# Six Strassen pairs in the last mLSTM heads and eight in the attention of a two-layer encoder trunk

## The chip, the cores and the metric

The kernel runs on one core of one Trainium2 chip. The metric is device time in microseconds (us) of one launch. Five engines run their own instruction streams in order and meet at semaphores: TensorE (PE in the profile, with its weight loads as PEld), VectorE (DVE), ScalarE (ACT), GpSimd (POOL, unused here) and SyncE (SP), whose queue issues every DMA of this kernel.

## The reference

One sequence of 512 tokens, width 2048, float32, passes two layers. Each layer normalises, modulates by a condition vector `c`, mixes, gates, projects back and adds a gated, normalised residual.

```python
# layer 0: mLSTM, 8 heads, dk 256, dv 512; w_in 2048 x (2*2048 + 3*4096 + 16)
qk = silu(causal_conv(proj[..., :A_V0], conv_w, conv_b))        # q and k, 8 heads x 256 each
ht = mlstm_chunkwise(q, k, v, li, lf)                           # gated linear attention
y = sigmoid(o) * rmsnorm_per_head(ht, g_head) * silu(z)
x = x + gate * rmsnorm(y @ w_out, g_post)                       # w_out 4096 x 2048
# layer 1: band attention, 16 heads x 128, K and V from the stream after layer 0
kv = modulated(rmsnorm(x, kv_g)) @ kv_w                         # 2048 x 4096
qz = modulated(rmsnorm(x, g_pre)) @ b_w_in                      # 2048 x 4096: queries and gate z
o = chunk_band_attention(q, k, v, rel_table)                    # softmax(q k / sqrt(128) + bias)
x = x + gate * rmsnorm((o * silu(z)) @ w_out, g_post)           # 2048 x 2048
```

## The kernel before

**Arithmetic.** All products are float32 made of float32r matmuls. `split` (L181 on ACT, L182 on DVE) cuts a float32 tile into a rounded high part (`wh` for weights) and the rest (`wl`). `mm3` issues three matmuls, high x high, high x low and low x high, so one 128 x 128 weight block costs three matmuls per 256 or 512 tokens.

**Weights.** `stream()` lists the weight matrices as pieces of up to 128 x 1024 floats, in the order of use. `wpiece` loads the next piece into `wr` (tag `raw`, two buffers, a third from a pool named in `spare` in some stages), then splits it into `wh` and `wl` (three buffers each). Loads, splits and results are traced with a priority 300 instructions ahead; a planner in the framework then fixes one order for each engine and inserts the semaphores. A tile pool has so many buffers for a tag; an instruction that writes a tile whose buffer is still read waits for the last reader.

**Seven products.** `proj_s` computes two column tiles c1, c2 of 128 outputs each, from 16 row tiles of 128 taken as eight pairs. For a pair the 2 x 2 grid of weight blocks meets two row tiles and two halves of 256 tokens. The plain way (`eight` in the code) takes 4 x `mm3` of 512 tokens, 12 matmuls. Strassen's way in Winograd's form (`seven`) takes 7 x `mm3` of 256 tokens, 21 matmuls, with sums of weight blocks and sums of token halves as operands. The argument `f` says how many of the eight pairs go the Strassen way; the rest go the plain way. Four PSUM tiles D, C, A, B collect the products, and an evacuation (L313 on ACT, L314 to L322 on DVE) adds them up into z1 and z2; PSUM has five such tiles, so the next tile's C, A and B take over the buffers of the last tile's D, C and A.

**Sums of weights.** For each Strassen pair `wpiece` computes on DVE L206, L207 (in place, in the raw tile) and L208 into `ws`, and splits `ws` into `wsh` and `wsl`. A piece holds either one Strassen pair and one plain pair, or two Strassen pairs. With `merged=True` two pairs share one `ws` tile of 768 columns (keys and attention); without it each pair has its own of 384 (heads). `bufs=(2, 3)` in the heads means two buffers of `ws` and three of `wsh` and `wsl`; a `wsh` buffer is free again when PE has finished the A product of its pair.

**Stages.** From 0 to about 243 us the condition vector, the norms and the projections of the first heads (`lead`, `ps_l`) run together. Heads 0 to 3 of the mLSTM use plain projections, with sums for the condition (L381) on DVE in the background. From head 4 (`HALF`) the o and z columns go through `proj_s` with `RAMP = [4, 5, 5, 5]` pairs, one number for each of the four tiles, while `head_sums` builds the token sums; heads 5, 6 and 7 use `HEAD_PAIRS = 5` for q, k and the four o/z tiles, six tiles a head. A head runs q tile, k tile, v (plain), four o/z tiles. Its end, the products `ps_n` with v, the squares, a reciprocal of a 128 x 512 tile (L737) and four multiplies (L739), runs beside the q tile of the next head. `nm` is a row of gate values broadcast over partitions (L655), read by L657 and by the exponentials L601 and L603; `v3` is the fourth quarter of v, read by the last `ps_n` matmul of each group.

Then come `a_w_out`, the residual, K and V (`proj_s` for K with 6, 7 and then 8 pairs, merged, sums in pool `zp`), and the inputs `h2`, with `three_sums` for each Strassen pair of the attention. The attention loop has one `proj_s` for each of 16 heads with `ATT_PAIRS = 7`, giving q (scaled, split into `q`) and the gate z (`z`, two buffers holding both). At the third piece `mid()` runs for older heads: `mixed(h-2)` (products with v, `ps_o`; result times z, L1046; store to `y2c`), `weights(h-1)` (scores `ps_s`, bias and maximum L1010, exponentials L1011, reciprocal L1012, scaling L1013) and the loads `fetch_k(h + 1)`, `fetch_v(h)` on SP. K of a head is split into `k` at the end of `queries`, and its first 128 columns are read as they are by the first score matmul of `weights`. Last comes `b_w_out` and the second residual.

Of the kernel before, what the change touches and what calls it, by code (L numbers as in the profile page):

```python
# [9 lines left out]
F32 = mybir.dt.float32  # L10
F32R = mybir.dt.float32r
# [4 lines left out]
P = 128  # L16
D = 2048
S = 512
# [9 lines left out]
BH = 16  # L28
# [12 lines left out]


KEY_PAIRS = [6, 7, 8, 8, 8, 8, 8, 8]
HEAD_PAIRS = 5
RAMP = [4, 5, 5, 5]
HALF = NH // 2
ATT_PAIRS = 7


def pair_pieces(f, merged=False):  # L50
# [82 lines left out]
def hybrid_trunk(ctx, tc, xT, xN, c, adaT, cols, wst, wg, ext, kc, out):  # L133
    nc = tc.nc
# [8 lines left out]
    def pool(name, bufs=1, **kw):  # L143
        return tc.tile_pool(name=name, bufs=bufs, reuse_waits="tile", **kw)
# [9 lines left out]
    ksc = [dram.tile([P, 2, S], F32, name=f"ksc{i}") for i in range(BH // 2)]  # L154
    vsc = [dram.tile([P, 4, S], F32, name=f"vsc{g}") for g in range(4)]
# [24 lines left out]
    def split(hi, lo, src):  # L180
        nc.scalar.copy(hi, src)  # L181
        nc.vector.tensor_tensor(lo, src, hi.bitcast(F32), op=ALU.subtract)  # L182
# [82 lines left out]
    def proj_s(mat, xs, ss, f, z1, z2, name, pl, bufs, at={}, merged=False):  # L265


        D, C, A, B = [newp(f"ps_{n}{name}") for n in "dcab"]
        pieces = pair_pieces(f, merged)
        begun = set()  # L270
        h0, h1_ = slice(0, 256), slice(256, 512)
        for i, (sk, nk) in enumerate(pieces):
            if i in at:
                at[i]()
            main, *extra = wpiece(mat, [len(ks) for ks in sk], pl, bufs)

            def acc(ps, cols, parts, b, x, last):
                start = id(ps) not in begun
                begun.add(id(ps))
                w = slice(b * P, (b + 1) * P)  # L280
                mm3(ps[:, cols], parts[0][:, w], parts[1][:, w], x[:, 0, :], x[:, 1, :], start, last)

            def eight():
                b0 = 4 * sum(len(ks) for ks in sk)
                for m, k in enumerate(nk):
                    for j in range(2):
                        for t, ps in enumerate((A, B)):
                            acc(ps, slice(0, S), main, b0 + 4 * m + 2 * j + t, xs[2 * k + j], False)

            def seven(g, ks):  # L290
                ns = len(ks)
                b0 = 4 * sum(len(u) for u in sk[:g])
                end = i == len(pieces) - 1 and g == len(sk) - 1
                for ps, cols, t, at_, x, last in (
                    (D, h1_, 0, 1, lambda k: ss[k][1], False),
                    (D, h0, 0, 0, lambda k: xs[2 * k][:, :, h0], end),
                    (C, h0, 1, 1, lambda k: ss[k][2], False),
                    (C, h1_, 1, 0, lambda k: ss[k][0], end),
                    (A, h0, 0, 3, lambda k: xs[2 * k + 1][:, :, h0], False),
                    (A, h1_, 1, 2, lambda k: xs[2 * k + 1][:, :, h1_], end),  # L300
                    (B, h0, 0, 2, lambda k: ss[k][3], end),
                ):
                    if i == 0 and g == 0 and ps is B:
                        eight()
                    for j, k in enumerate(ks):
                        acc(ps, cols, extra[g] if t else main, (0 if t else b0) + at_ * ns + j, x(k), last and j == ns - 1)

            if i:
                eight()
            for g, ks in enumerate(sk):  # L310
                seven(g, ks)
        with tc.high_priority(AHEAD):
            nc.scalar.copy(z1[:, 0, :], D[:, h0])  # L313
            nc.vector.tensor_tensor(z2[:, 1, :], z1[:, 0, :], D[:, h1_], op=ALU.add)  # L314
            nc.vector.tensor_tensor(z1[:, 1, :], z2[:, 1, :], C[:, h0], op=ALU.add)
            nc.vector.tensor_tensor(z2[:, 0, :], z2[:, 1, :], C[:, h1_], op=ALU.add)
            nc.vector.tensor_tensor(z2[:, 1, :], z1[:, 1, :], C[:, h1_], op=ALU.add)
            nc.vector.tensor_tensor(z1, z1, A.rearrange("p (a t) -> p a t", a=2), op=ALU.add)
            if f < KT // 2:
                nc.vector.tensor_tensor(z2, z2, B.rearrange("p (a t) -> p a t", a=2), op=ALU.add)  # L320
            else:
                nc.vector.tensor_tensor(z2[:, 0, :], z2[:, 0, :], B[:, h0], op=ALU.add)  # L322
# [37 lines left out]


    phA = ExitStack()
    tp = phA.enter_context(pool("t1", bufs=4, side="right"))
    mst = ExitStack()
    q1p = mst.enter_context(pool("q1", side="right"))
    ap_ = mst.enter_context(pool("ada", side="right"))
# [5 lines left out]
    sp = spare[0] = st.enter_context(pool("start"))  # L372
# [19 lines left out]
        return [ada_load(k, j, sp, 4) for j in range(2)] + [ada_load(KT + k, j, ap_, ADA_BUFS) for j in range(2)]  # L392

    pin = tc.keep_in_program_order
    crow = [tp.tile([P, S], F32, tag="t", name=f"crow{i}")[0:1] for i in range(4)]
    for i in range(4):
        pin(nc.sync.dma_start(crow[i], c[i * S : (i + 1) * S].unsqueeze(0)))
    xt, xq = [], []
# [1 line left out]
    for q in range(4):  # L400
        t = sp.tile([P, 4, S], F32, name=f"xt{q}")
# [44 lines left out]
    h1 = []  # L446
# [27 lines left out]
    hp = hst.enter_context(pool("head"))  # L474
# [98 lines left out]
    h1s = []  # L573
# [9 lines left out]

    def pair(c, name, f=HEAD_PAIRS, at={}):
        z1, z2 = (acp.tile([P, 2, 256], F32, tag="so", name=f"{name}_{i}", bufs=6) for i in range(2))
        proj_s("a_w_in", h1, h1s, f, z1, z2, name, hq, (2, 3), at)
        return [z.rearrange("p a t -> p (a t)") for z in (z1, z2)]

    def scores(h, j, qk, pr, nm, nmd, tot):
# [30 lines left out]
    for h in range(NH):  # L620
# [20 lines left out]
        if h == HALF:  # L641
# [5 lines left out]
            hq = hqst.enter_context(pool("hq", side="right"))  # L647
# [25 lines left out]
        for m in range(4):  # L673
            with tc.high_priority(AHEAD):
                if m < 3:
                    t = hp.tile([P, 2, S], F32R, tag="qk", name=f"v{h}_{m}", bufs=4)
                    split(t[:, 0, :], t[:, 1, :], pv[m])
                else:
                    t = hp.tile([P, S], F32, tag="v3", name=f"v{h}_{m}")
                    nc.scalar.copy(t, pv[m])  # L680
            v.append(t)
        if h < HALF:
# [239 lines left out]
    rst.close()  # L922
    zst = ExitStack()
    zp = zst.enter_context(pool("zp", bufs=2, side="right"))
    for i in range(KT // 2):
        z = zp.tile([P, 4, 256], F32, tag="z", name=f"zk{i}")
        ready = len(hs)
        at = {2: input_sums} if ready < KT // 2 else {}
        assert ready == KEY_PAIRS[i]
        spare[0] = zp  # L930
        proj_s("kv_w", hkv, hs, ready, z[:, 0:2, :], z[:, 2:4, :], f"k{i}", zp, (2, 2), at, True)
        nc.sync.dma_start(ksc[i].rearrange("p a t -> p (a t)"), z.rearrange("p a t -> p (a t)"))
    kst.close()
    ast = ExitStack()
    kq = ast.enter_context(pool("kq"))
# [26 lines left out]
    bias = at.tile([P, S], F32, name="bias")  # L962
    nc.vector.memset(bias[:64, 448:512], NEG)

    def fetch(h, ts, src, tag):
        ts.append(at.tile([P, S], F32, tag=tag, name=f"{tag}{h}", bufs=2))
        nc.sync.dma_start(ts[h], src)

    def fetch_k(h):
        fetch(h, kt, ksc[h // 2][:, h % 2, :], "kt")  # L970

    def fetch_v(h):
        fetch(h, vt, vsc[h // 4][:, h % 4, :], "vt")

    fetch_k(0)

    def queries(h, steps):

        z = at.tile([P, 4, 256], F32, tag="z", name=f"z{h}", bufs=2)
        proj_s("b_w_in", h2, h2s, ATT_PAIRS, z[:, 0:2, :], z[:, 2:4, :], f"z{h}", kq, (2, 2), steps, True)  # L980
        qz = z.rearrange("p a t -> p (a t)")
        nc.scalar.mul(qz[:, :S], qz[:, :S], P**-0.5)
        q = at.tile([P, 2, 384], F32R, tag="q", name=f"q{h}", bufs=2)
        split(q[:, 0, :], q[:, 1, :], qz[:, P:S])
        sz = qz[:, S:]
        nc.scalar.activation(sz, sz, AF.Silu)
        k = at.tile([P, 2, S], F32R, tag="kk", name=f"k{h}")
        split(k[:, 0, :], k[:, 1, :], kt[h])
        b0 = bsc[h]
        for p0, n in ((0, 448), (64, S)):  # L990
            src = bass.AP(b0.tensor, b0.offset + P - 1 + p0 * (EXTW - 1), [[EXTW - 1, 64], [1, n]])
            nc.sync.dma_start(bias[p0 : p0 + 64, :n], src)
        return (qz[:, :P], q, k), sz

    def weights(h, q0, q, k):

# [53 lines left out]
    for h in range(BH + 2):  # L1050

        def turn():
            if h > 1:
                pts[h - 2] += flipped(h - 2, prs.pop(h - 2), (2, 3))
                vs[h - 2] = split_v(h - 2)

        def mid():
            if h > 1:
                mixed(h - 2, pts.pop(h - 2), vs.pop(h - 2), szs.pop(h - 2))
            if 0 < h <= BH:  # L1060
                prs[h - 1] = weights(h - 1, *qs.pop(h - 1))
            if h < BH - 1:
                fetch_k(h + 1)
            if h < BH:
                fetch_v(h)

        if h < BH:
            qs[h], szs[h] = queries(h, {1: turn, 2: mid})
        else:
            turn()  # L1070
            mid()
        if 0 < h <= BH:
            pts[h - 1] = flipped(h - 1, prs[h - 1], (0, 1))
# [105 lines left out]
```

## Time and profile before

| quantity | value |
|---|---|
| three runs | 2814.0, 2814.4, 2812.62 us; median 2814.0 us |
| the profiled execution's own time | 2812.05 us, 1.75 us more than its span |
| its span, first to last instruction | 2810.3 us |
| mean granted TensorE clock | 0.998 |
| busy PE / DVE / ACT | 2777.9 / 2059.0 / 1330.2 us |
| attention, one head | 25.24 us, start to start |

A row of a timeline gives start, duration (us), engine, source line, operation, output <- input, shapes and how many; in square brackets the idle time before it and what ended it. Matmuls overlap, so the distance of two starts is the cost, not the duration. A row of a window gives for each engine its busy time and its instructions. A row of the waits gives the sum of a wait, how often, and the longest.

### The profile page before, as it was taken

Reading aid. Unit: us, or ns where it says so; the run is one execution under the profiler, and the core shown is the slowest. Engines: PE = TensorE matmul, PEld = TensorE weight load, DVE = VectorE, ACT = ScalarE, POOL = GpSimd, SP = SyncE. Lnnn points to the kernel's source line nnn. Section 1 sums busy time; section 2 is a strip of 40 time slices with the busy share of each in tenths; the row PEclk is TensorE's granted clock in tenths of the full one; section 3 lists DMA queues with packets and bytes.
Section 4 is the critical chain, followed back from the end, with each engine's and each line's share of the span. In section 5 each row is a group of like instructions: output and inputs, shape, how many; then the busy total and the mean of one; then the engine's idle time right before and its main releaser. Section 6 shows DMA issues by size and latency. Waiting matters only on the chain.

```text
span 2810.3 us, 40423 instructions
## 1 busy us (share of the span) xinstructions
PE 2777.9 (99%) x15308; PEld 2420.7 (86%) x15308; DVE 2059.0 (73%) x3473; ACT 1330.2 (47%) x1955; POOL 0.2 (0%) x4
## 2 busy tenths in 40 slices
PE   7999999999999999999999999999999999999998
PEld 5787888888888989989988888888998899999887
DVE  7986978868689776856867445567985788889625
ACT  4234524234334554444635344568534466666523
POOL 0000000000000000000000000000000000000000
PEclk9999999999999999999999999999999999999999
DMA  8875687868774332332323656788535534334635
GB/s 300 299 257 182 222 319 242 307 221 285 263 241 154 106 113 90 110 100 99 109 91 133 223 195 209 256 265 298 176 129 173 171 123 127 120 127 127 229 102 171
DMA packets 177371, 524.33 MB, mean 187 GB/s; under 512 B 19044, under 2 KB 37508, under 8 KB 176664
## 3 DMA queue, kind: packets, MB, share of 16 engines
q1 hardware_dynamic: 177176, 521.75, 55.0%
q8 instruction: 120, 1.97, 0.3%
q14 instruction: 75, 0.61, 0.1%
HBM read 488.07 MB, written 38.85 MB: 187 GB/s over the span
## 4 chain that ended last, share of the span: by engine, by line
PE 89%; DVE 5%; DMA 3%; issue 2%; ACT 1%; SPq 0%; DVEq 0%; ACTq 0%
PE ps_y L223 18%; PE ps_v L223 10%; PE ps_o L223 6%; PE ps_z L223 5%; PE ps_azo L223 4%; PE ps_qk L223 4%; PE ps_az L223 4%; PE ps_bzo L223 3%; PE ps_l L223 3%; PE ps_kv L223 3%; PE ps_cz L223 3%; PE ps_dz L223 3%; PE ps_bz L223 2%; PE ps_s L223 2%; PE ps_czo L223 2%; PE ps_dzo L223 2%
## 5 line engine op out<-in xcount | busy, mean ns | idle before, releaser
L182 DVE TENSOR_TENSOR wl<-wr,wh 128x1024 fp32r<-128x1024 f32 (+3 forms) x586 | 678.3, 1159 | 410.5 <-ACT wh L181 400.4
L181 ACT CAST wh<-wr 128x1024 fp32r<-128x1024 f32 (+3 forms) x586 | 585.8, 1000 | 819.1 <-PE ps_y L223 231.7
L223 PE MATMUL ps_y<-wh,y 128*128 128x512 f32 x1536 | 475.6, 390 | 0.0
L223 PEld LDWEIGHTS ps_y<-wh,y 128*128 128x128 f32 x1536 | 288.3, 188 | 59.5
L223 PE MATMUL ps_v<-wh,h 128*128 128x512 f32 x1024 | 321.7, 390 | 0.0
L181 ACT CAST wsh<-ws 128x384 fp32r<-128x384 f32 (+1 forms) x205 | 129.5, 632 | 368.7 <-issue 132.1
L223 PE MATMUL ps_y<-wl,y 128*128 128x512 f32 x768 | 299.0, 389 | 0.0
L182 DVE TENSOR_TENSOR wsl<-ws,wsh 128x384 fp32r<-128x384 f32 (+1 forms) x205 | 144.1, 703 | 122.6 <-ACT wsh L181 122.6
L223 PEld LDWEIGHTS ps_v<-wh,h 128*128 128x128 f32 x1024 | 192.2, 188 | 39.5 <-issue 0.3
L223 PE MATMUL ps_v<-wl,h 128*128 128x512 f32 x512 | 199.7, 390 | 0.0
L381 DVE CUSTOM_DVE_ANT_0 ada<-ada,scB,mod 128x1024 f32<-128x1024 f32 x128 | 163.9, 1280 | 26.1 <-DMA ada<-in_adaT 24.6
L381 DVE CUSTOM_DVE_ANT_0 ada<-ada,scB,cl 128x1024 f32<-128x1024 f32 x128 | 163.6, 1279 | 20.6 <-DMA ada<-in_adaT 20.2
L223 PEld LDWEIGHTS ps_y<-wl,y 128*128 128x128 f32 x768 | 144.2, 188 | 29.8
L223 PE MATMUL ps_kv<-wh,hkv 128*128 128x512 f32 x512 | 159.7, 391 | 0.0
L206 DVE TENSOR_TENSOR ws<-wr 128x256 f32<-128x256 f32 (+1 forms) x205 | 104.7, 520 | 30.3 <-DMA wr<-in_wst 28.3
L223 PE MATMUL ps_qk<-h,wh 128*128 128x512 f32 x384 | 119.2, 390 | 0.0
L223 PE MATMUL ps_o<-h,wh 128*128 128x512 f32 x384 | 118.2, 389 | 0.0
L223 PE MATMUL ps_z<-h,wh 128*128 128x512 f32 x384 | 118.2, 389 | 0.0
L223 PEld LDWEIGHTS ps_v<-wl,h 128*128 128x128 f32 x512 | 96.2, 188 | 19.9 <-issue 0.9
L223 PEld LDWEIGHTS ps_kv<-wh,hkv 128*128 128x128 f32 x512 | 95.9, 188 | 19.6
L223 PE MATMUL ps_l<-h,wh 128*128 128x512 f32 x320 | 99.4, 392 | 1.6 <-ACT oz L467 0.9
L223 PE MATMUL ps_kv<-wl,hkv 128*128 128x512 f32 x256 | 99.7, 389 | 0.0
(385 smaller groups left out, 5865.4 us busy)
## 6 DMA issues: line engine op xcount, KB each, us to landing
wr<-in_wst SPq DMA_DIRECT2D x520, 512.0 KB, 3.4
ada<-in_adaT SPq DMA_DIRECT2D x256, 512.0 KB, 5.8
xt<-nsc SPq DMA_DIRECT2D x46, 256.0 KB, 4.0
yr<-ysc SPq DMA_DIRECT2D x16, 512.0 KB, 3.6
wr<-in_wst SPq DMA_DIRECT2D x30, 256.0 KB, 3.8
wr<-in_wst SPq DMA_DIRECT2D x16, 384.0 KB, 5.7
bsc<-in_ext SPq DMA_DIRECT2D x16, 320.0 KB, 5.8
xt<-in_xT SPq DMA_DIRECT2D x4, 1024.0 KB, 7.0
```

The lines of the kernel that those rows point to most:

```text
L181: nc.scalar.copy(hi, src)
L182: nc.vector.tensor_tensor(lo, src, hi.bitcast(F32), op=ALU.subtract)
L206: nc.vector.tensor_tensor(t[:, : 2 * w], r[:, w : 3 * w], r[:, : 2 * w], op=ALU.subtract)
L223: nc.tensor.matmul(ps, a, b, start=start, stop=stop)
L381: pin(nc.vector.tensor_tensor_reduce(at, at, scB[:, j * D // 2 : (j + 1) * D // 2], 1.0, mod[:, i : i + 1] if j else col(CB + i), ALU.mult ...
```

## The change

`HEAD_PAIRS` goes from 5 to 6, the last two tiles of `RAMP` from 5 to 6, and `ATT_PAIRS` from 7 to 8. That is one more Strassen pair in 18 tiles of heads 5 to 7, in 2 tiles of head 4 and in 16 of the attention: 36 pairs. More token sums (`h1s`, `h2s`) must be held. Room for them is taken from: one of four buffers of pool `t1` (temporaries of the whole first layer; one of the four `crow` tiles moves to pool `start`); one of three `wsh` and `wsl` buffers in the heads; the buffer of `v3`, which now shares `nm`'s single buffer; and in the attention one of two buffers for K (`kt`), one of two for the split query (`q`), and one of two for the raw query, by cutting `z` into `zq` (one buffer) and `z` (two). K of head h is now loaded in `mid()` of head h and not of head h - 1. The weight sums of the key stage get a pool of their own (`zx`) that is closed before the last values.

```diff
-HEAD_PAIRS = 5
-RAMP = [4, 5, 5, 5]
+HEAD_PAIRS = 6
+RAMP = [4, 5, 6, 6]
 HALF = NH // 2
-ATT_PAIRS = 7
+ATT_PAIRS = 8
...
-    tp = phA.enter_context(pool("t1", bufs=4, side="right"))
+    tp = phA.enter_context(pool("t1", bufs=3, side="right"))
...
-    crow = [tp.tile([P, S], F32, tag="t", name=f"crow{i}")[0:1] for i in range(4)]
+    crow = [(tp if i < 3 else sp).tile([P, S], F32, tag="t", name=f"crow{i}")[0:1] for i in range(4)]
...
-        proj_s("a_w_in", h1, h1s, f, z1, z2, name, hq, (2, 3), at)
+        proj_s("a_w_in", h1, h1s, f, z1, z2, name, hq, (2, 2), at)
...
-                    t = hp.tile([P, S], F32, tag="v3", name=f"v{h}_{m}")
+                    t = hp.tile([P, S], F32, tag="nm", name=f"v{h}_{m}")
...
+    zxst = ExitStack()
+    zx = zxst.enter_context(pool("zx", side="right"))
...
-        proj_s("kv_w", hkv, hs, ready, z[:, 0:2, :], z[:, 2:4, :], f"k{i}", zp, (2, 2), at, True)
+        proj_s("kv_w", hkv, hs, ready, z[:, 0:2, :], z[:, 2:4, :], f"k{i}", zx, (2, 2), at, True)
...
+    zxst.close()
...
-        fetch(h, kt, ksc[h // 2][:, h % 2, :], "kt")
+        fetch(h, kt, ksc[h // 2][:, h % 2, :], "kt", 1)
...
-        z = at.tile([P, 4, 256], F32, tag="z", name=f"z{h}", bufs=2)
-        proj_s("b_w_in", h2, h2s, ATT_PAIRS, z[:, 0:2, :], z[:, 2:4, :], f"z{h}", kq, (2, 2), steps, True)
-        qz = z.rearrange("p a t -> p (a t)")
-        nc.scalar.mul(qz[:, :S], qz[:, :S], P**-0.5)
-        q = at.tile([P, 2, 384], F32R, tag="q", name=f"q{h}", bufs=2)
-        split(q[:, 0, :], q[:, 1, :], qz[:, P:S])
-        sz = qz[:, S:]
+        z1 = at.tile([P, 2, 256], F32, tag="zq", name=f"zq{h}")
+        z2 = at.tile([P, 2, 256], F32, tag="z", name=f"z{h}", bufs=2)
+        proj_s("b_w_in", h2, h2s, ATT_PAIRS, z1, z2, f"z{h}", kq, (2, 2), steps, True)
+        zq, sz = (z.rearrange("p a t -> p (a t)") for z in (z1, z2))
+        nc.scalar.mul(zq, zq, P**-0.5)
+        q = at.tile([P, 2, 384], F32R, tag="q", name=f"q{h}")
+        split(q[:, 0, :], q[:, 1, :], zq[:, P:])
...
-            if h < BH - 1:
-                fetch_k(h + 1)
+            if 0 < h < BH:
+                fetch_k(h)
```

More of the change, by code (lines that the diff above doesn't have):

```diff
@@ L963, in hybrid_trunk, with fetch @@
     nc.vector.memset(bias[:64, 448:512], NEG)
-    def fetch(h, ts, src, tag):
-        ts.append(at.tile([P, S], F32, tag=tag, name=f"{tag}{h}", bufs=2))
+    def fetch(h, ts, src, tag, bufs):
+        ts.append(at.tile([P, S], F32, tag=tag, name=f"{tag}{h}", bufs=bufs))
         nc.sync.dma_start(ts[h], src)
     def fetch_k(h):
-        fetch(h, kt, ksc[h // 2][:, h % 2, :], "kt")
+        fetch(h, kt, ksc[h // 2][:, h % 2, :], "kt", 1)
     def fetch_v(h):
-        fetch(h, vt, vsc[h // 4][:, h % 4, :], "vt")
+        fetch(h, vt, vsc[h // 4][:, h % 4, :], "vt", 2)
     fetch_k(0)
     def queries(h, steps):
-        z = at.tile([P, 4, 256], F32, tag="z", name=f"z{h}", bufs=2)
-        proj_s("b_w_in", h2, h2s, ATT_PAIRS, z[:, 0:2, :], z[:, 2:4, :], f"z{h}", kq, (2, 2), steps, True)
-        qz = z.rearrange("p a t -> p (a t)")
-        nc.scalar.mul(qz[:, :S], qz[:, :S], P**-0.5)
-        q = at.tile([P, 2, 384], F32R, tag="q", name=f"q{h}", bufs=2)
-        split(q[:, 0, :], q[:, 1, :], qz[:, P:S])
-        sz = qz[:, S:]
+        z1 = at.tile([P, 2, 256], F32, tag="zq", name=f"zq{h}")
[5 more added lines that the diff above has]
+        split(q[:, 0, :], q[:, 1, :], zq[:, P:])
         nc.scalar.activation(sz, sz, AF.Silu)
@@ L992, in queries @@
             nc.sync.dma_start(bias[p0 : p0 + 64, :n], src)
-        return (qz[:, :P], q, k), sz
+        return (zq[:, :P], q, k), sz
     def weights(h, q0, q, k):
```

## The prediction

> **What bounds the kernel now.** I read the page's busy shares first, then the chain of waits, then what PE waits for. The four fields of a window row are busy time and instruction counts of PE, PEld, DVE, ACT and POOL, then the clock, the DMA share and GB/s.
>
> ```profile
> span 2810.3 us, 40423 instructions
> ...
> PE 2777.9 (99%) x15308; PEld 2420.7 (86%) x15308; DVE 2059.0 (73%) x3473; ACT 1330.2 (47%) x1955; POOL 0.2 (0%) x4
> ...
> PE 89%; DVE 5%; DMA 3%; issue 2%; ACT 1%; SPq 0%; DVEq 0%; ACTq 0%
> ```
> ```profile
> PE ps_lead L223 <- ACT h L358: 8.9, 4, 3.4
> ...
> PE ps_az L223 <- DVE h L182: 0.8, 1, 0.8
> ```
> ```profile
> 985.00:995.00 10.00, 10.00 (x62) 8.91 (x61) 8.90 (x14) 4.17 (x7) 0.00 (x0) 1.00 0.15 53
> 995.00:1005.00 10.00, 10.00 (x75) 9.51 (x74) 9.68 (x18) 3.81 (x6) 0.00 (x0) 1.00 0.56 176
> 1005.00:1015.00 10.00, 10.00 (x64) 9.02 (x63) 9.93 (x20) 5.50 (x7) 0.00 (x0) 1.00 0.32 106
> 1255.00:1275.70 20.70, 20.70 (x143) 19.23 (x142) 12.66 (x27) 7.24 (x12) 0.00 (x0) 1.00 0.31 102
> 2107.00:2214.00 107.00, 107.00 (x580) 93.26 (x579) 66.65 (x111) 46.44 (x66) 0.00 (x0) 1.00 0.52 173
> 2301.71:2326.95 25.24, 25.24 (x193) 24.35 (x192) 22.40 (x49) 16.20 (x30) 0.00 (x0) 1.00 0.39 125
> ```
>
> PE is busy for 99% of the span and its largest wait belongs to the start. So a removed matmul is worth its full time, as long as nothing else takes PE's place. The DVE column says where something might. In an attention head (last row) DVE has 2.84 us of 25.24 left, and beside the q and k tiles of a late head (first three) only 1.49 of 30. In an o/z tile (1255) and in the last values (2107) it has room.
>
> **The matmuls saved.** The rows are starts of PE in one attention head: a piece of two Strassen pairs begins at 2285.12 and ends at 2290.16; a plain pair runs from 2293.08 to 2295.83.
>
> ```profile
> 2285.12 0.40 PE L223 MATMUL ps_dz<-h2s,wh 128*128 128x256 f32 x2
> ...
> 2290.16 0.93 PE L1023 MATMUL ps_t<-kcs,s 128*128 128x128 f32 x7
> 2290.85 0.48 PE L223 MATMUL ps_dz<-h2s,wh 128*128 128x256 f32 x2
> ...
> 2293.08 0.63 PE L223 MATMUL ps_az<-h,wh 128*128 128x512 f32 x2
> ...
> 2295.83 0.40 PE L223 MATMUL ps_bz<-h2s,wh 128*128 128x256 f32 x2
> ```
>
> Plain: 12 matmuls of 512 tokens, 2.75 us, 229 ns each. Strassen: 42 matmuls of 256 for two pairs in 5.04 us, so 21 in 2.52, 120 ns each. The gain is 0.23 us a pair, and 36 pairs give **-8.3 us** (20 in the heads -4.6, 16 in the attention -3.7). Loads and bytes of weights stay the same. The Trainium skill speaks against this change: "TensorE: Matmul & The Clock Gate", section "Back-to-back issue gap", gives a sustained spacing of about 81 ns at 128 columns and 131 ns at 512. A straight line between them is 98 ns at 256, an estimate, by which a pair would go from 1.57 to 2.06 us and 36 pairs would cost 17 us. The rows above, 229 and 120 ns, time the very matmuls and decide against that; no chance is given to it.
>
> **Attention: the single K buffer.** rows of SP, ACT and DVE in a head's middle and end, and between them the times that the 16 loads of `kt` took from issue to landing:
>
> ```profile
> 2279.74 0.38 SPq L967 DMA_DIRECT2D kt<-ksc  x1
> ```
> ```profile
> DMA to landing us min/median/max: 4.4/6.2/6.5
> ```
> ```profile
> 2282.34 0.60 ACT L181 CAST k<-kt 128x512 fp32r<-128x512 f32 x1
> ```
> ```profile
> 2283.69 0.67 DVE L182 TENSOR_TENSOR k<-kt,k 128x512 fp32r<-128x512 f32 x1
> 2284.28 0.48 DVE L1013 TENSOR_SCALAR s<-s,mx 128x512 f32<-128x512 f32 x1
> 2285.08 0.56 DVE L182 TENSOR_TENSOR wsl<-ws,wsh 128x384 fp32r<-128x384 f32 x1 [0.33 <-ACT wsh L181]
> 2285.68 0.69 DVE L206 TENSOR_TENSOR ws<-wr 128x512 f32<-128x512 f32 x1
> ...
> 2289.21 0.41 DVE L317 TENSOR_TENSOR z<-z,ps_cz 128x256 f32<-128x256 f32 x1
> ...
> 2298.82 0.41 DVE L206 TENSOR_TENSOR ws<-wr 128x256 f32<-128x256 f32 x1
> 2299.27 0.29 DVE L207 TENSOR_TENSOR wr<-ws,wr 128x128 f32<-128x128 f32 x1
> ```
>
> Before, the K issued at 2279.74 is for the next head and has a whole head to land. After, `mid()` issues it at the same place for the same head. Landing at 2285.94 (+6.2), ACT's cast cannot start at 2282.34 but ends at 2286.54. DVE, in order, has finished the softmax at about 2284.15 (2284.28 + 0.48 less the 0.6 of `k` itself), so it sits idle for 2.4 us with the split of `k`, the split of the next tile's first sums, `wl` and the evacuation L314 to L322 queued behind it; on ACT the `wsh` and `wh` casts queue too. DVE also gets more work from the eighth pair: L206, L207 and L208 and the split of the fourth piece take the wide form (0.69 for 0.41, twice 0.42 for 0.29, 0.96 for 0.56), and the last addition shrinks from 0.69 to 0.41: +0.67 us. Its cycle is 22.40 + 0.67 + 2.4 = 25.47 us, or about 25.07 if five of its short gaps close up (0.08 each, an estimate from the 0.2 to 0.33 us gaps in these rows). PE's is 25.24 - 0.23 = 25.01. DVE exceeds it by 0.06 to 0.46 us; over the 15 heads with this load 0.9 to 6.9 us. From that comes once what PE has in hand: from the start of `k` to the end of L317 took 5.9 us, 5.4 without the L1013 between, so after the cast's end at 2286.54 L317 would end near 2292.0, while the next head's A, which takes its PSUM buffer, starts 24 matmuls after 2290.85, near 2293.8: 1.8 us. The loss is 0 to 5.1; I take **+1.9**, from the middle of the excess (15 x 0.25 - 1.8), since some gaps will close.
>
> The Trainium skill's "DMA: Bandwidth & Descriptors", section "Anatomy of one DMA — SWDGE (gpsimd) path", has about 2.0 us plus bytes over 436 GB/s, for transfers issued from GpSimd: 2.6 us for these 256 KB, an estimate. By it K would be there at 2282.3, with no idle time and the full 3.7 us kept. The median of 16 landings, 6.2 us, decides for the loss.
>
> **q and k tiles of heads 5 to 7.** DVE at the end of the head before, beside the q tile:
>
> ```profile
> 993.12 3.35 DVE L737 RECIPROCAL dd<-dd 128x512 f32<-128x512 f32 x1 [0.72 <-ACT dd L736]
> ```
>
> Each of these tiles gets L206, L207, L208 and one more split: 0.41 + 0.29 + 0.29 + 0.56 = 1.55 us of DVE work. In the 30 us of the three windows above DVE has 1.49 us to spare and gets 3.1, while PE saves 0.46. A deficit of up to 2 us is partly covered by the pieces split ahead. With two `wsh` buffers, not three, that cover shrinks: the fourth piece's split must wait for PE's A product of the third piece's first pair, and if that falls behind the reciprocal, 3.35 us of DVE stand in front of it. I take 1.0 us a head between 0 (cover holds) and 2 (it doesn't): **+3.0** for three heads, 0 to 6.
>
> **o/z tiles with six pairs.** There are 14 (12 in heads 5 to 7, two in head 4). Window 1255 leaves DVE 8 us of 20.7, so 1.55 more hides. Two buffers delay the fourth piece's split behind an A product; in the order of placement D of the second piece now often stands ahead of A of the first, which gives PE other work meanwhile. I take 0.05 each between 0 and 0.2: **+0.7**.
>
> **Pool `t1`, four buffers to three.** Nothing in the trace shows this wait. Its nearest row is the wait of 8.9 us above, four times in the start, where PE isn't full. If one temporary of heads 0 to 4 came late by a 512-token DVE operation (0.68 us), twice, it would be 1.4. I take **+0.4** of 0 to 1.5; a gain is excluded, as fewer buffers release nothing earlier.
>
> **`v3` in `nm`'s buffer.** `nm` now waits on SP until the last `ps_n` of the previous head has read `v3`.
>
> ```profile
> 977.20 7.23 PE ps_n L223 x44
> ```
> ```profile
> 982.54 0.33 SPq L656 DMA_DIRECT2D ssum<-gsc  x1
> 992.43 0.33 SPq L199 DMA_DIRECT2D wr<-in_wst  x1
> ```
> ```profile
> nm<-gsc SPq DMA_DIRECT2D x8, 256.0 KB, 4.2
> ```
> ```profile
> 988.95 0.68 DVE L657 TENSOR_TENSOR nmd<-nm,maskd 128x512 f32<-128x512 f32 x1
> ```
>
> The products end at 984.43, 1.9 us after the load's place in the queue. It lands at 988.6 (+4.2), 0.3 before L657 wants it, and the next weight load on SP is not due before 992.43. **0**, at most 0.5 a head.
>
> **First attention head.** Its first piece held a plain pair of the last `h`, which is what PE waits for there (0.8 us, second of the waits quoted). That pair is gone, so **-0.5**, between 0 and -0.8. The `three_sums` that replace it are some 3 us on DVE, hidden in 2107 to 2214 with 40 us free. If the sums come last there instead, the wait stays.
>
> **Edits at nothing.** `zq` and one `q` buffer are free again in `mid()`, about 10 us before the next head writes them. The pool `zx` only ends earlier than `zp` did; its readers are long done.
>
> **Sum.** -8.3 + 1.9 + 3.0 + 0.7 + 0.4 - 0.5 = -2.8 us. The profiled execution took 2812.05 us (1.75 around its span), so 2809.2. The median of the runs lies 1.95 above that execution: **2811.2**.
>
> **The rivals.**
>
> *All hidden.* The K landing is a median under a weight load issued 1 us earlier. If it lands within 25.01 - 23.07 = 1.94 us of DVE idle, that is in 5.75 us or less (the fastest took 4.4), or if DVE's gaps close by 0.46, the attention loses nothing; if the pieces split ahead cover the q and k tiles too, what is left is -8.3 - 0.5 + 0.4 = -8.4: 2805.6. For it speaks that excess and cover are both fractions of a us; against it DVE's 9.93 of 10 us.
>
> *Slower: K becomes the bound of the attention.* The cycle is then the K load, ACT's cast and DVE's queue behind it, and each us of landing is a us per head. The other terms sum to -4.7, so it is slower than 0.2% (5.6 us) once 15e - 1.8 - 4.7 exceeds 5.6, at an excess of e = 0.81 us, a landing of 6.6 us if no gap closes, 7.0 if five do. The longest seen is 6.5. With e = 1.0: +8.5 and 2822.5. For it speaks how near 6.5 is; against it that the same queue carries the same bytes.
>
> *Slower: two `wsh` buffers stop PE in every head tile.* If PE comes to the fourth piece before its split, each q and k tile would lose its 1.55 us of new DVE work, 6 x 1.5 = 9, and each o/z tile about a split's 0.56, 14 x 0.5 = 7. With -6.5 for the rest: +9.5 and 2823.5. Against it stands DVE's room in 1255.
>
> **How the numbers follow.** The forecast (part of the gain given back) has 0.38, all hidden 0.34, K the bound 0.18, the buffers 0.10. A measurement of this kernel tells about 0.2%, 5.6 us, from no change: faster is below 2808.4, slower above 2819.6. The forecast's own range is 2808 to 2817 (K +5.1 and head tiles +6 not both at their worst), inside "same" but for its edge. So faster 0.34, same 0.38, slower 0.28. For 8 in 10 the range goes from the hidden case, 2805.0, to near the K case, 2821.5.
>
> **What the profile after would show.** 432 fewer 512-column matmuls and 756 more of 256. A head period in the attention of 25.01 us if hidden, over 25.1 if DVE sets it; an ACT wait for `kt` fifteen times, DVE idle before `k` near 2.4 us. PE waits for `wl`, `wh` or `wsl` in the q and k tiles of heads 5 to 7, and PE below 10 of 10 in those windows; no PE wait for `h` in the first attention head. I am wrong if the K wait is absent or several us longer, if PE stops in o/z tiles, or if the `t1` temporaries make PE wait in heads 0 to 4.

## The result and the profile after

| | before | after |
|---|---|---|
| median of 7 runs | 2814.0 us | 2821.9 us (2818.8 to 2826.5) |
| ratio to before | | 1.0033, 95% interval 1.0021 to 1.0045 |
| profiled execution, span | 2810.3 us | 2824.7 us |
| PE busy in the span | 99% | 98% |

The change is slower by 7.9 us, where 2811.2 us was forecast and 2821.5 was the end of the range. The profiled execution after took 2826.5 us, the slowest of its seven, so the profiles stand 14.4 us apart; a second profile of the same kernel (below) shows which part of that is chance of one execution.

The page of the kernel after:

```profile
span 2824.7 us, 41212 instructions
...
PE 2782.3 (98%) x15632; PEld 2433.5 (86%) x15632; DVE 2095.3 (74%) x3567; ACT 1348.1 (48%) x1981; POOL 0.2 (0%) x4
...
PE 81%; DVE 9%; DMA 4%; issue 3%; ACT 2%; SPq 0%; DVEq 0%; ACTq 0%
```

The matmuls went as planned (324 more in number), but the chain's share of PE fell from 89 to 81%. Where it went is seen by stage. The rows of the windows are, in both kernels: the first o/z tile of head 4 to the first product of `a_w_out`; the body of the attention (first to last product of the 16 tiles); its end (to the last product with v, beside the first products of the last projection); the last projection. Columns as in the prediction: PE, PEld, DVE, ACT, POOL, clock, DMA share, GB/s. Before:

```profile
891.57:1526.97 635.40, 633.83 (x3932) 573.77 (x3931) 453.92 (x856) 315.44 (x442) 0.00 (x0) 1.00 0.31 104
...
2221.10:2618.08 396.98, 396.22 (x3004) 382.23 (x3002) 347.05 (x751) 251.14 (x431) 0.00 (x0) 1.00 0.42 130
2618.08:2634.70 16.62, 16.42 (x92) 13.79 (x91) 14.94 (x37) 14.77 (x30) 0.00 (x0) 1.00 0.65 239
2634.70:2800.34 165.64, 165.64 (x734) 137.13 (x732) 66.36 (x77) 52.86 (x76) 0.00 (x0) 1.00 0.46 159
```

After:

```profile
890.93:1526.02 635.09, 632.28 (x4112) 579.09 (x4111) 477.72 (x940) 323.99 (x460) 0.00 (x0) 1.00 0.31 104
...
2228.13:2623.19 395.06, 392.86 (x3147) 386.51 (x3146) 350.36 (x747) 254.78 (x431) 0.00 (x0) 1.00 0.42 130
2623.19:2643.08 19.89, 18.00 (x93) 14.94 (x92) 15.60 (x37) 14.51 (x30) 0.00 (x0) 0.91 0.58 199
2643.08:2814.85 171.77, 169.36 (x733) 138.87 (x732) 67.44 (x79) 53.97 (x78) 0.00 (x0) 0.98 0.46 156
```

Of the gain forecast for the matmuls, heads 4 to 7 kept 0.3 of 4.6 us and the body of the attention 1.9 of 3.7. The end of the attention is 3.3 us longer and the last projection, which the change does not touch, 6.1. Both show a clock below 1.00. PE's waits in these three stages, and how the tile `kt` was waited for:

```profile
PE ps_t L1026 <- DVE pt L182: 1.9, 1, 1.9
PE ps_s L223 <- DVE z L1049: 1.9, 3, 1.2
PE ps_y L223 <- ACT wh L181: 1.1, 1, 1.1
PE ps_y L223 <- DVE wl L182: 0.8, 1, 0.8
PE ps_y L223 <- ACT y L181: 0.5, 1, 0.5
```
```profile
  DMA kt<-ksc: 50.2, 15
  ACT k L181: 32.7, 15
...
DMA to landing us min/median/max: 3.8/6.0/6.6
```

The first two rows of the second fence are the idle time until K landed and until ACT's part of `k` was done, and how often: ACT waits 3.3 us a head and DVE 2.2, fifteen times, close to the forecast 2.4. In the end of the attention the same wait is followed by a stop of PE (`ps_t`, 1.9 us).

**The end and the half clock.** After the last tile's K, the rows of DVE, SP and ACT in the kernel after:

```profile
2620.46 0.69 DVE L182 TENSOR_TENSOR k<-kt,k 128x512 fp32r<-128x512 f32 x1 [2.97 <-ACT k L181]
2621.41 1.23 DVE L182 TENSOR_TENSOR wl<-wr,wh 128x1024 fp32r<-128x1024 f32 x1 [0.26 <-ACT wh L181]
...
2628.20 1.48 DVE L182 TENSOR_TENSOR pt<-ps_t,pt 128x512 fp32r<-128x512 f32 x3
```
```profile
2622.67 3.43 SPq L199 DMA_DIRECT2D wr<-in_wst  x3
```
```profile
2625.97 1.05 ACT L181 CAST wh<-wr 128x1024 fp32r<-128x1024 f32 x1 [2.19 <-DMA wr<-in_wst]
```

The split `wl` of a weight piece stands behind `k` on DVE. When it ends (2622.64), SP issues the next load of weights; ACT waits 2.19 us for it, and `pt` on DVE stands behind the split of the piece that it brings. With K a head ahead (below) the same `wl` ended 2.45 us before the tile's last product, here 0.55 us. PE waits for `pt`:

```profile
2628.94 0.33 PE L1026 MATMUL ps_t<-kcs,s 128*128 128x128 f32 x1 [1.89 <-DVE pt L182]
...
2629.86 3.00 PE L223 MATMUL ps_o<-pt,vv 128*128 128x512 f32 x9
...
2641.40 1.73 PE L223 MATMUL ps_o<-pt,vv 128*128 128x512 f32 x9
```

After the stop the nine `ps_o` products take 3.00 us, a head later the same nine 1.73. The trace's record of the granted clock has 0.5 for 3.4 us from 2629.2 on, and for 6.8 us from 2670.2 on. The second follows a stop in the last projection:

```profile
2668.77 0.50 PE L223 MATMUL ps_y<-wh,y 128*128 128x512 f32 x1 [1.13 <-ACT wh L181]
2670.03 0.69 PE L223 MATMUL ps_y<-wl,y 128*128 128x512 f32 x1 [0.76 <-DVE wl L182]
```

10.2 us at half clock are up to 5.1 us of lost products, an estimate (half of the time, though PE also stood still in a part of it), where PE's waits in the end and the last projection are 4.3 us together. By these rows PE waits at the second stop for weights, `wh` and `wl`, and only 0.5 us for `y`; what brings it about is found on SP's queue. The load of the seventh `y2` tile stood directly ahead of the first load of `x2` before, at 2636.34. After, it stands behind the eight loads of `x2` and four loads of weights, 41 us after the last projection's first product (2624.2), not 17 (2619.1):

```profile
2636.34 0.32 SPq L1094 DMA_DIRECT2D y2r<-y2c  x1
```
```profile
2664.58 0.33 SPq L199 DMA_DIRECT2D wr<-in_wst  x1
2664.95 0.91 SPq L1097 DMA_DIRECT2D y2r<-y2c  x2
```

The planner, which gives each engine one order, laid out the end of the attention differently once K came late, and put this load elsewhere. The profiles of all the runs below agree: in the four profiles where the last head's K is late and this load is not moved it stands behind all of `x2`, in the eight where that K comes a head ahead it stands ahead of `x2`. That the order causes the second stop is shown by moving the load back (below).

### The profile page after: what moved, and what is told of

It is laid out like the page before. It is cut to its first block, busy times and chain, and to the rows that moved or that the text cites. A ratio compares the mean times of both kernels' runs of the same rounds, so it can differ in the third digit from the quotient of the medians.

```text
span 2824.7 us, 41212 instructions
## 1 busy us (share of the span) xinstructions
PE 2782.3 (98%) x15632; PEld 2433.5 (86%) x15632; DVE 2095.3 (74%) x3567; ACT 1348.1 (48%) x1981; POOL 0.2 (0%) x4
## 4 chain that ended last, share of the span: by engine, by line
PE 81%; DVE 9%; DMA 4%; issue 3%; ACT 2%; SPq 0%; DVEq 0%; ACTq 0%
PE ps_y L223 17%; PE ps_v L223 10%; PE ps_o L223 5%; PE ps_z L223 5%; PE ps_qk L223 4%; PE ps_kv L223 3%; PE ps_azo L223 3%; PE ps_l L223 3%; PE ps_cz L223 3%; PE ps_dz L223 3%; PE ps_az L223 2%; DVE wl L182 2%; PE ps_bzo L223 2%; PE ps_dzo L223 2%; PE ps_czo L223 2%
## 5 line engine op out<-in xcount | busy, mean ns | idle before, releaser
L181 ACT CAST wsh<-ws 128x384 fp32r<-128x384 f32 (+1 forms) x225 | 144.9, 644 | 258.0 <-issue 126.9
L182 DVE TENSOR_TENSOR wsl<-ws,wsh 128x384 fp32r<-128x384 f32 (+1 forms) x225 | 161.4, 717 | 80.2 <-ACT wsh L181 79.1
L206 DVE TENSOR_TENSOR ws<-wr 128x256 f32<-128x256 f32 (+1 forms) x225 | 117.2, 529 | 24.7 <-DMA wr<-in_wst 23.0
```

Of the source, the lines that this page charges most:

```text
L206: nc.vector.tensor_tensor(t[:, : 2 * w], r[:, w : 3 * w], r[:, : 2 * w], op=ALU.subtract)
```

## The experiments

**The changed kernel once more**, for a second profile.

> The changed kernel once more, for a second profile. Its first profile was the slowest of its seven runs (2826.5, median 2821.9). If the 7.4 us between a_w_out and the key stage come from the change, they are there again (Rival B); if they are chance of one execution, these stages take 353 and 91 us as before. The half-clock stretches in the last projection (10 us together, some 5 us of time): theory 1 says that they follow a stop of PE at the end of the attention, so at least one is there again.

Median 2822.9 us, ratio 1.0031 (1.0019 to 1.0042). Per stage: heads 4 to 7 636.5, body 395.2, end 20.3, last projection 172.0 us, with half-clock stretches of 3.4 and 6.8 us at the same two places. `a_w_out` took 355.4 us (before 353.0, first profile after 355.7); the values after it 92.0 (before 91.3, first profile after 96.0). So `a_w_out`'s 2.3 to 2.7 us belong to the change, and of the 4.7 us in the values some 4 are chance of one execution: Rival B holds for a part only. Over all profiles the values take 92.0 to 96.0 us with six pairs in every late head and 91.3 to 93.6 with five.

**Head edits alone.**

```diff
-HEAD_PAIRS = 5
-RAMP = [4, 5, 5, 5]
+HEAD_PAIRS = 6
+RAMP = [4, 5, 6, 6]
... (and the edits of t1, crow, (2, 2) and v3; attention as before)
```

> Only the head edits (six pairs in the 18 + 2 tiles, t1 with three buffers, two wsh and wsl buffers, v3 in nm's buffer); the attention is that of the kernel before. Theory 1 (the late K load of the attention makes the change slow; the head edits cost about what they save): between the first o/z tile of head 4 and the first product of a_w_out the two profiles differ by 0.3 us where 20 pairs x 0.23 = 4.6 were saved, so this run is 1 us faster than before, -3 to +1 us. Rival A (the head edits are the cause): +5 us or more. Rival B (the stages between, a_w_out to the last values, which were 8 us longer in the profile after with the same order of instructions, are slowed by the new layout of memory): here too these stages are 7 us longer.

Median 2817.0, ratio 1.0012 (1.0003 to 1.0021): 2.8 us slower, between theory 1 and Rival A. Rival B's 7 us behind the heads came as 5.7 in this profile, 2.2 of them in `a_w_out` and 2.95 in the values. Head 5 in three rows (q and k tiles; v; four o/z tiles), before and here:

```profile
984.19:1026.40 42.21, 42.21 (x288) 39.15 (x286) 35.81 (x60) 19.43 (x27) 0.00 (x0) 1.00 0.34 116
1026.40:1073.89 47.49, 47.49 (x218) 39.68 (x217) 27.27 (x45) 23.31 (x34) 0.00 (x0) 1.00 0.28 95
1073.89:1164.78 90.89, 90.89 (x611) 84.38 (x610) 65.28 (x137) 46.10 (x63) 0.00 (x0) 1.00 0.30 101
```
```profile
981.68:1023.83 42.15, 42.15 (x305) 39.69 (x304) 38.83 (x74) 22.24 (x33) 0.00 (x0) 1.00 0.39 125
1023.83:1072.16 48.33, 47.86 (x218) 39.54 (x217) 28.39 (x48) 23.04 (x33) 0.00 (x0) 1.00 0.31 99
1072.16:1162.24 90.08, 90.08 (x647) 85.53 (x646) 67.09 (x145) 45.99 (x65) 0.00 (x0) 1.00 0.28 94
```
```profile
PE ps_v L223 <- DVE zq L318: 1.7, 3, 0.8
PE ps_q L223 <- ACT sp_q L181: 1.5, 2, 1.2
```

The o/z tiles gained 0.81 of 0.92 us. The q and k tiles gained 0.06 of 0.46, although PE is busy for all of 42.15 us and its waits have none there: the starts of PE show gaps of about 0.1 us over the usual spacing at the first D products of a piece, 0.5 us together. The v products lost 0.84: the first of them wait until DVE, late from the k tile, has added up the PSUM tile that they take over (L318). At the start of `a_w_out` PE waits for `sp_q`, the squares of head 7's end (`ps_q`).

**The rooms of the heads without the pairs, and the third `wsh` buffer alone.** The first has t1, crow, (2, 2) and v3 with five pairs; the second only:

```diff
-        proj_s("a_w_in", h1, h1s, f, z1, z2, name, hq, (2, 3), at)
+        proj_s("a_w_in", h1, h1s, f, z1, z2, name, hq, (2, 2), at)
```

> The kernel before with the head edits that make room (t1 with three buffers, two wsh and wsl buffers, v3 in nm's buffer) but with five pairs. Theory 2 (the lost gain of the heads is DVE work of the added sums beside the q and k tiles): q and k tiles take 42.2 us as before and v 47.5; only the 1.3 us at the start of a_w_out and the 1.0 us at the turned rows, seen in all four profiles with the head edits, are there: +2 to +3 us. Rival D (it is the missing buffers that stop PE in the heads): q, k and v together 0.7 to 1.5 us longer a head, so +4 to +7 us.

> The kernel before with two wsh and wsl buffers in the heads and nothing else. The run with all three edits for room and five pairs lost 0.2 us in each q and k stretch and 0.6 us in the four o/z tiles of a head, 2 us in all. Theory 4: that is the third buffer: q and k 42.4, o/z 91.5, +1.5 to +2.5 us. Rival G (t1 or v3): 42.2 and 90.9 as before, 0 us.

2817.4 us, 1.0012 (1.0003 to 1.0020), and 2816.7, 1.0010 (1.0001 to 1.0020). Both show the same stretches: q and k 42.40 us, v 47.49, o/z 91.5. In the run with two buffers alone the o/z row is

```profile
1072.51:1164.02 91.51, 91.51 (x612) 84.55 (x610) 65.62 (x133) 45.78 (x61) 0.00 (x0) 1.00 0.30 99
```

0.62 us longer than before's 90.89. So theory 4 holds: of the three edits for room only the missing `wsh` buffer costs, and `t1` and `v3` add nothing that can be seen (Rival G falls). In the first run neither forecast came out: q, k and v lost 0.2 us a head, less than Rival D's 0.7 to 1.5, but the o/z tiles 0.6, where Theory 2 had no loss. Its `a_w_out` took 353.0 us as before, not longer, so the longer time comes with the added pairs. Why 1 us of it lies at the transposes of the stream (L830, where PE waits for `xn` of DVE) was not tried.

**Attention edits alone.** The attention of the changed kernel with the heads of before.

> Only the attention edits (eight pairs, one buffer for K and its load half a head later, one q buffer, zq, zx); the heads are those of the kernel before. Theory 1: the body of the attention keeps 1.9 of 3.7 us, its end (from the last piece of the last tile to the last product with v) loses 3.3, and the last projection, starved at its start, loses some us more: +2 to +8 us against before. Rival A (the heads are the cause): -2 us or less. Rival B: the stages from a_w_out to the last values are 7 us longer than before's again only if it is zx that does it.

2824.8 us, 1.0038 (1.0025 to 1.0050). Body 394.7, end 21.7, last projection 173.7 us, with half-clock stretches of 3.4 and 6.8 us. `a_w_out` 353.1, and the stages from there to the last values 3.3 us longer than before, not Rival B's 7. The run is 10.5 us slower than before, above Theory 1's 2 to 8: its mechanism stands, its size was too small. The attention alone makes the change slow.

**K a head ahead, with all other edits.**

```diff
-        fetch(h, kt, ksc[h // 2][:, h % 2, :], "kt", 1)
+        fetch(h, kt, ksc[h // 2][:, h % 2, :], "kt", 2)
...
-                    t = at.tile([P, n], F32, tag=f"pt{j}", name=f"pt{h}_{j}")
+                    t = at.tile([P, n], F32, tag="s0", name=f"pt{h}_{j}")
...
-            if 0 < h < BH:
-                fetch_k(h)
+            if h < BH - 1:
+                fetch_k(h + 1)
```

> The changed kernel with K in two buffers again and loaded a head ahead, as before (room: the 128 x 128 tile pt3 shares the buffer of s0). Theory 1: the wait of ACT for kt goes, the head period in the attention falls to 25.0 us, the end of the attention takes 20.2 us again: -3.7 in the attention, -1 in the heads, so 4 to 5 us faster than before, 2809. Rival A: the heads still cost, so +3 us or more. Rival B: stages between still 7 us longer, so +3 us or more as well, but with the time there.

2809.9 us, 0.9987 (0.9978 to 0.9996), 12 us faster than the changed kernel and 4 faster than before. Its waits for `kt` and its three stages:

```profile
  DMA kt<-ksc: 3.1, 1
```
```profile
2222.53:2615.19 392.66, 392.66 (x3148) 386.77 (x3146) 352.02 (x750) 255.16 (x431) 0.00 (x0) 1.00 0.43 132
2615.19:2631.99 16.80, 16.55 (x92) 13.88 (x91) 14.96 (x38) 14.71 (x30) 0.00 (x0) 1.00 0.65 241
2631.99:2797.61 165.62, 165.62 (x734) 137.18 (x732) 66.38 (x77) 52.85 (x76) 0.00 (x0) 1.00 0.48 159
```

The late K costs 2.4 us in the body (395.06 - 392.66), 3.1 at the end and 6.15 in the last projection, 11.6 together in these profiles. From the third head on a head takes 25.03 us here, each of them; with late K 25.0 to 25.5, and one 26.3, whose 1.2 us of PE waiting for `z` (`ps_s`, above) are half of the body's loss.

**Late K alone**, in the kernel before (seven pairs, other buffers as they were).

```diff
-        ts.append(at.tile([P, S], F32, tag=tag, name=f"{tag}{h}", bufs=2))
+        ts.append(at.tile([P, S], F32, tag=tag, name=f"{tag}{h}", bufs=1 if tag == "kt" else 2))
...
-            if h < BH - 1:
-                fetch_k(h + 1)
+            if 0 < h < BH:
+                fetch_k(h)
```

> The kernel before with one edit: K of the attention in one buffer and loaded in mid() of its own head; seven pairs, the other buffers as they were. Theory 1 (the late K costs by its place, at the end of the attention above all): the body is about as before, since DVE's cycle is 22.40 + 2.4 = 24.8 us under PE's 25.24, the end of the attention takes 3 to 5 us more (18.9 and 20.7 for 15.6 in the runs with late K), the last projection 6 us more, with half-clock stretches after PE's stop: +9 to +11 us. Rival C (a late K costs only beside the eighth pair's DVE work): 0 to +1 us, the end as before.

2821.6 us, 1.0029 (1.0017 to 1.0040).

```profile
2225.20:2622.63 397.43, 396.31 (x3003) 382.31 (x3002) 343.46 (x749) 251.10 (x431) 0.00 (x0) 1.00 0.42 129
2622.63:2640.64 18.01, 16.52 (x93) 13.81 (x91) 14.98 (x36) 13.95 (x28) 0.00 (x0) 1.00 0.59 218
2640.64:2812.04 171.40, 168.03 (x734) 138.18 (x732) 67.42 (x79) 53.98 (x78) 0.00 (x0) 0.99 0.47 157
```

Rival C falls: 8.0 us slower. ACT waits 49.6 us for K here as well, and the body hardly loses (+0.45 us): DVE has the room, 343 of 397 us busy. The end loses 1.4 us, less than the 3 to 5 forecast, and the last projection 5.8, without an eighth pair anywhere. The last projection has 3.4 us at half clock from 2669.8 on; the end has none. The key stage, which the edit does not touch, is 4.1 us longer in this profile, with 3.4 us at half clock, and is not counted here.

**One load moved back on SP's queue**, in the changed kernel.

```diff
-            nc.sync.dma_start(raw, y2c[i])
+            with tc.high_priority(900 if i == 6 else 0):
+                nc.sync.dma_start(raw, y2c[i])
```

> The changed kernel with one edit in the last projection: the load of the seventh y2 tile gets a higher priority, so that on SP's queue it stands behind the first load of x2, not behind all eight and five loads of weights. K stays late. In the kernels with late K it stood there because the planner laid out the end of the attention differently. Theory 3 (the 6 us lost in the last projection are this order: y2 lands late, PE stops for 2.4 us, and a stretch of 3.4 or 6.8 us at half clock follows): the last projection takes 165.6 us again, so 4.5 to 6.5 us faster than the changed kernel, 2816 to 2818, with the end of the attention still at 18.9. Rival E (the late K itself delays the last results, and the order is only a sign of it): the last projection stays above 170 us.

2820.1 us, 1.0018 (1.0009 to 1.0027).

```profile
2226.42:2621.56 395.14, 392.88 (x3147) 386.50 (x3146) 350.28 (x748) 254.60 (x431) 0.00 (x0) 1.00 0.42 130
2621.56:2641.58 20.02, 17.94 (x93) 15.08 (x92) 15.50 (x37) 14.31 (x29) 0.00 (x0) 0.91 0.58 198
2641.58:2808.41 166.83, 166.22 (x734) 136.97 (x732) 67.56 (x79) 53.97 (x78) 0.00 (x0) 1.00 0.48 161
```

The last projection falls from 171.8 to 166.8 us and its half-clock stretch is gone, while body and end stay. Rival E falls, and Theory 3 holds for 5 of the 6 us in the profile; the medians moved by 1.8 to 2.8 us (2821.9 and 2822.9 to 2820.1), less than the 4.5 forecast, so how much of the 5 us holds over many runs is not settled.

**Only the last head's K early**, in the changed kernel.

```diff
-        fetch(h, kt, ksc[h // 2][:, h % 2, :], "kt", 1)
+        fetch(h, kt, ksc[h // 2][:, h % 2, :], "kl" if h == BH - 1 else "kt", 1)
...
-            if 0 < h < BH:
+            if 0 < h < BH - 1:
                 fetch_k(h)
+            if h == BH - 2:
+                fetch_k(h + 1)
... (and pt3 in s0's buffer, as above)
```

> The changed kernel, with K of the last head alone in a buffer of its own and loaded one head ahead (pt3 shares s0's buffer); K of heads 1 to 14 stays late. Theory 1 in its present form (2.5 us in the body from 14 late heads, 9.5 us at the end from the last head and the order that follows from it): body 395, end 15.6 to 16.5, last projection 165.6, so 2812 to 2813. Rival F (the lag of DVE built up over the body is what makes the end long): end still 18 us or more, 2816 or more.

2814.9 us, 1.0002 (0.9993 to 1.0011).

```profile
2226.32:2622.37 396.05, 392.86 (x3147) 386.49 (x3146) 351.39 (x749) 255.22 (x431) 0.00 (x0) 1.00 0.42 130
2622.37:2639.86 17.49, 16.64 (x92) 13.80 (x91) 15.08 (x38) 14.79 (x30) 0.00 (x0) 1.00 0.61 228
2639.86:2805.97 166.11, 166.11 (x734) 136.98 (x732) 66.40 (x77) 52.79 (x76) 0.00 (x0) 1.00 0.48 159
```

Fourteen late heads cost 3.4 us against all early (396.05 to 392.66); the one last head, and the order that follows from it, cost 8 (19.89 + 171.77 down to 17.49 + 166.11). The run is some 2 us above its forecast, and the end 1 us above the 16.5. The end stays under Rival F's 18, so the lag of DVE built up over the body is at most a small part of it.

**Versions that might beat both.** K ahead in the attention with the heads of before, and K ahead with six pairs in the o/z tiles but five in q and k.

> The heads of the kernel before, and the attention with eight pairs and K loaded a head ahead. Theory 1: the attention's body is 4.3 us shorter (392.7 for 397.0, as in the run with all edits and K ahead), the rest as before: 4 us faster than before, 2810; and if the head edits cost 2.8 us as they did alone, 2807. It beats the run with the head edits by up to 3 us if the costs add up, and is equal if not.

> The kernel with K loaded a head ahead and eight pairs in the attention, six pairs in the o/z tiles, but five again in the q and k tiles. Theory 2: q and k tiles back at 42.2 us, which is what they took with six pairs, v at 47.5 instead of 48.1 to 48.4, o/z still at 90.0: 1 to 2.5 us faster than the one with six pairs there, 2808. Rival D: v still 48.2, so no faster.

2810.9 us, 0.9991 (0.9982 to 1.0000), and 2812.7, 0.9998 (0.9989 to 1.0007). The first keeps the whole gain of the attention (body 392.6) and nothing else, as forecast. The second, forecast at 2808, was no better than six pairs throughout, as Rival D had it: its q and k stretches took 42.43 us, v 47.5 to 48.1. The 42.4 is what the two `wsh` buffers alone gave. Whether the head edits gain or lose beside K ahead (2809.9 or 2810.9) is within the intervals and stays open; by the profiles they cost 1.4 us from head 4 to the end of `a_w_out`.

## Why the prediction was wrong

- **The gain of the matmuls** was right in the attention: with K ahead the body went from 396.98 to 392.66 us, 4.3, where 3.7 plus the 0.5 of the first head's wait were forecast, and that wait (`ps_az` for `h`) is gone.
- **"Attention: the single K buffer", +1.9 us, is the step that failed.** Its mechanism was seen as forecast: 6.0 us median landing, DVE idle 2.2 us before `k`, heads of 25.0 to 25.5 us (one 26.3), 2.4 us lost in the body. But the sum ran over 15 heads as if a next tile stood behind each of them, and stopped there. After the last tile there is little to hide the wait: the end lost 3.1 us. And the term took the order around it as given. The planner laid out the end anew for the late K, a load of `y2` went behind twelve others on SP, and the last projection lost 6.15 us, of which moving that one load gave back 5 in the profile. Measured, the term is 11.6, not 1.9; the medians, 2821.9 against 2809.9, say 12.0.
- **The rival "K becomes the bound of the attention"** came to 2822.5, near the measured 2821.9, but not by its mechanism: the landing was 6.0 us in the median and never above the 6.6 that it needed in every head, the body lost 2.4 us in all, and late K alone cost 8 us with no eighth pair. That the number fits is luck. The 2.6 us estimated from the Trainium skill's "DMA: Bandwidth & Descriptors", section "Anatomy of one DMA — SWDGE (gpsimd) path", for transfers issued from another engine, did not come: every K in the kernel after took 3.8 us or more.
- **q and k tiles, +3.0.** Too small, and wrong in part about the place. In the kernel after, the q and k stretches of heads 5 to 7 lost the 1.4 us of gain, and 0.7 more, most of it in one wait for head 5's end. The signs forecast for it hardly show: PE is busy there all but 0.5 of 127 us, and of waits for `wl`, `wh` or `wsl` only the weight loads have one, for `wh`, of 0.2 us a head. Another 0.4 to 0.9 a head went in v (head 5: 48.4 for 47.5), where DVE's lag comes out and no cost was forecast; with five pairs in q and k, v took 47.5 to 48.1. Nor was a cost forecast in `a_w_out` (1.7 to 2.7 us longer with six pairs; some 0.9 us of waiting stood in head 7's o/z tiles before, which got 1.85 us shorter, where the pairs give 0.92). From head 4 to the end of `a_w_out` the head edits cost 2.4 us alone, and 2.4 and 3.5 in the two profiles of the changed kernel, where -0.9 was forecast.
- **o/z tiles, +0.7.** With six pairs about right: 0.77 to 0.88 of 0.92 us a head gained in heads 5 and 6, and nothing in the two tiles of head 4 (92.85 us for 92.62 from its first o/z tile to head 5). With five pairs the missing `wsh` buffer costs 0.62 a head in these tiles and 0.2 in q and k, some 2.4 us in all, as the third rival said, but far under its 16.
- **`t1`, `v3`, `zq`, one `q` buffer**: nothing that can be seen, as forecast for the last three (0.4 for `t1` was too much).

## What to carry to other kernels

A transfer moved from a head ahead to the same head was mostly hidden in the middle of the loop by the work around it, and showed at the loop's end, where little is left to hide it: cost the last turn by itself. In a kernel whose queues are laid out by a planner, a delay also changes the order of what comes after it; compare the order of SP's loads before and after, past the stage that was edited. And where room is needed, look for a tile to share whose reader is long done: with one 128 x 128 tile in another's buffer the second K buffer stayed, and a loss of 8 us became a gain of 4.

## What the runs showed of the hardware

A short stop of PE cost more than its length. In the kernel after, a gap of 2.3 us between two starts of PE at 2626.7 was followed by a granted clock of 0.5 for 3.4 us, and gaps of 1.5 and 1.3 us from 2667.3 on by 6.8 us of it, into which a third gap of 1.2 us fell. A gap of 2.1 us at 1910.1 in the same kernel brought none, nor did one of 1.9 us at 2626 with late K alone. In the key stage gaps of 1.8 and 1.0 us within four us (late K alone), or 1.6 and 1.0 (two `wsh` buffers alone), brought 3.4 us at half clock from 1997.3 on, and 1.5 and 1.0 (all rooms of the heads) none.

The traces show what sorts these cases. In each of the thirteen profiles the changes of the granted clock lie whole multiples of 3.413 us apart, so a profile can be cut into windows of that length. As an estimate of a window's idle time, add up what the distances of PE's starts have over the usual spacing (0.12 us at 256 columns, 0.23 at 512). From 95 us to the last product, all eight windows at full clock with over 2.2 us of idle time were followed by half clock, four of the seven with 1.95 to 2.15 us, and none of some 10,000 with less. A gap of 4.2 us in the run of the attention edits alone is cut by a window's edge into two of about 2.0, and half clock came only behind the second. The Trainium skill, "TensorE: Matmul & The Clock Gate", section "HAM oscillation — how this bites in real kernels", gives as the rule that PE should have no idle gaps above about 3.4 us. As a bound on one gap that differs from these runs, where a gap of 2.3 us, or gaps of 1.6 and 1.0 us together, were enough; the stretches themselves last 3.4 us or twice that. By the windows, these runs put the bound near 2 us of idle time in 3.4.
